# Linear attention in three parts: scores of a pair of blocks, outputs of the preceding pair, projections of the next; W_o's pieces by single chunks

## The chip, the cores and the metric

The kernel runs on one core of a Trainium2 chip. The metric is the device time of one execution in microseconds (us). Engines are named TensorE (PE in the profile; PEld is its weight load), VectorE (DVE), ScalarE (ACT), GpSimd (POOL) and SyncE (SP, which here only issues DMAs).

## The reference

One step of a hybrid decoder layer, in float32. A prompt of 2048 tokens and 8 decoded tokens pass through a normalisation and one combined projection. One half of the projected columns feeds sliding-window attention, the other half gated linear attention. Their outputs go through W_o, are added to the input, and a SwiGLU feed-forward layer follows.

```python
def gla_chunked(q, k, v, log_a, s0):
    """S_t = diag(a_t) S_{t-1} + k_t^T v_t, o_t = q_t S_t, chunk by chunk"""
    ...
    def step(S, inp):
        qc, kc, vc, ac = inp
        b = jnp.cumsum(ac, axis=2)
        o_inter = jnp.einsum('nhtd,nhdv->nhtv', qc * jnp.exp(b), S)
        diff = b[:, :, :, None, :] - b[:, :, None, :, :]
        decay = jnp.exp(jnp.where(causal[:, :, None], diff, -jnp.inf))
        scores = jnp.einsum('nhtd,nhsd,nhtsd->nhts', qc, kc, decay)
        o = o_inter + jnp.einsum('nhts,nhsv->nhtv', scores, vc)
        b_last = b[:, :, -1:, :]
        S = (jnp.exp(b_last[:, :, 0, :, None]) * S
             + jnp.einsum('nhsd,nhsv->nhdv', kc * jnp.exp(b_last - b), vc))
        return S, o

def finish(x, o_attn, o_gla, r_gla, gla_norm_g, w_o, ffn_norm_g, w_gate, w_up, w_down):
    g = rmsnorm(o_gla, gla_norm_g).reshape(N, T, GLA_WIDTH) * jax.nn.silu(r_gla)
    h = x + jnp.concatenate([o_attn, g], axis=-1) @ w_o
    z = rmsnorm(h, ffn_norm_g)
    return h + (jax.nn.silu(z @ w_gate) * (z @ w_up)) @ w_down
```

There are 4 heads with 64 key and 128 value columns.

## The kernel before

The program has five stages, one after another: sliding-window attention (to about 405 us of the span), gated linear attention (about 405 to 750), the W_o product with the second normalisation (about 727 to 937), gate and up products, and the down product. The last two use Strassen's seven products. A float32 product is made of three matmuls with split operands (`mm3`, L105 to L109): `split` (L94 to L96) makes a high part on ScalarE and the remainder on VectorE.

All instructions of an engine run in the order in which they were placed when the program was built. The framework places them by a simulated timeline (L1443, `schedule_with_timeline_sim`): whatever can start first goes first, and of several candidates the one that stands earlier in the program. At run time each engine keeps that order and waits at its head. SyncE's DMA issues are such a queue too, and so are GpSimd's instructions. Tiles live in pools with a fixed number of buffers (`bufs`); a tile whose buffer is still being read waits for it.

Linear attention works on pairs of 128-token blocks, pp = 0 to 7. Two functions did the work, and the loop at L955 to L959 called `gla_b(pp)`, then a piece of the decoded tokens' work (`next(dec)`), then `front_b(pp + 1)`.

- `front_b(pp)`: the projections of a pair. It loads the pair's normalised input `zT` (2 MB, L682, two halves in turn), makes q and k (`ps_qk`, 96 matmuls of 256 columns), the gates (`ps_g`) with their running sum `Bt` (L730), and the values v (`ps_v`, 48 matmuls of 512 columns, L743). It also loads r, the output gate made in the first stage (L754).
- `gla_b(pp)`, first half: the scores. Seven levels (`LEVELS`, 64 down to 1). In each, VectorE subtracts the running sum at a boundary (L797), ScalarE takes the absolute value and exponential (L798, L799), GpSimd multiplies q into a block-diagonal operand `bd` (L811, two instructions), VectorE multiplies k into E (L812), TensorE makes the level's scores (`ps_l`, L816), and ScalarE (L821) or a masked copy of VectorE (L826) puts them into `AT`. Then come the diagonal `dg` (L834 to L836), q with decay `eB` (L838, L841), its last column `ebl`, and the decayed and transposed keys `kdN` (L844 to L853).
- `gla_b(pp)`, second half: the outputs, block by block. `po` sums AT times v (L865) and eB times the running state `Sbd` (L868); `pst` makes the state's addition (L873), which VectorE applies (L880). VectorE adds the diagonal (`ob`, L886), ScalarE squares (L891), GpSimd multiplies by r (L892) and takes the inverse root (`rstd`, L115), ScalarE scales (L896), TensorE transposes (`ps_m`, L900), and the result goes to DRAM as `mix_d` (L903).

W_o is split into high and low parts inside the linear attention, and stored in DRAM (`wo_d`) for the next stage. `split_wo(i, behind)` (L769) splits the raw piece loaded by its last call, writes it, and loads the next. It was called in levels 1 and 5 of pairs 1 to 5, each piece two chunks of 128 rows by 512 columns; its ScalarE instruction is ordered behind the level's exponential (L799). Its pool has one buffer for the raw piece and one for the result.

The next stage loads `wo_d` as soon as its space is free (L1026; part of it overlaps `zT`, which the last `ps_v` reads), the mixed outputs (`mr`, L1016) and the residual input `h` (L1021; its buffers lie where tiles of the linear attention lay). `ps_wo` has four accumulators, each read by L586 together with h.

Of the kernel before, what the change touches and what calls it, by code (L numbers as in the profile page):

```python
# [10 lines left out]
F32 = mybir.dt.float32  # L11
# [9 lines left out]
P = 128  # L21
# [30 lines left out]
def hymba_kernel(ctx: ExitStack, tc: tile.TileContext, I, O, X=None, phases=3):  # L52
# [521 lines left out]

    def load_wo(wr, k0, dh):

        cols = slice(dh * 512, dh * 512 + 512)
        v = wr.rearrange("p (k n) -> p k n", k=2)
        if k0 >= 4:
            return [(v, w_o[k0 * P:(k0 + 2) * P, cols].rearrange("(k p) n -> p k n", p=P))]  # L580
        return [(v[64 * h:64 * h + 64], w_o[h * 256 + k0 * 64:h * 256 + (k0 + 2) * 64, cols]
                 .rearrange("(k p) n -> p k n", p=64)) for h in range(2)]

# [8 lines left out]
    with ExitStack() as ph:  # L592
# [4 lines left out]
        dp = pool(ph, "b_dec", 1)  # L597
        lp = pool(ph, "b_lm", 1)
        gtp = pool(ph, "b_gt", 2)
# [42 lines left out]
        lmask = pad.tile([P, len(LEVELS) * 64], U8, name="lmask")  # L642
        lm = lp.tile([P, 528], F32, name="lm")[:, 0:len(LEVELS) * 64]
        nc.sync.dma_start(lm, I["c_lmask"])
# [32 lines left out]
        def front_b(pp):  # L677
# [55 lines left out]
            def values():  # L733
                vs, rs = [], []
                toks = [(0, P), (P, P)] + ([(256, ND)] if pp == 0 else [])
                for c0, n in toks:
                    ps = acc.tile([P, 512], F32, tag="acc", name="ps_v")
                    v = wk.tile([P, 512], F32, tag="v", name="v", bufs=4)
                    if n == P:
                        for k in range(KD):  # L740
                            mm3(ps, nT[:, 0, k, c0:c0 + n], nT[:, 1, k, c0:c0 + n], WV[:, 0, k], WV[:, 1, k],
                                k == 0, k == KD - 1)
                        nc.scalar.copy(v, ps)  # L743
                    else:
                        for k in range(KD):
                            for hl in range(2):
                                nc.tensor.matmul(ps[:40], nTdec[:, k], WV[:, hl, k], start=k == 0 and hl == 0,
                                                 stop=k == KD - 1 and hl == 1)
                        nc.scalar.copy(v[:n], ps[32:40])
                        nc.vector.tensor_tensor(v[:n], ps[:n], v[:n], ALU.add)  # L750
                    vs.append(v)
                    if n == P:
                        r = wl.tile([P, 512], F32, tag="r", name="r", bufs=4)
                        nc.sync.dma_start(r, r_d[2 * pp + c0 // P])  # L754
                        rs.append(r)
                return vs, rs

            la, Bt = gates()
            vs, rs = values()
            if pp == 0:  # L760
# [3 lines left out]
                nc.sync.dma_start(vdec_d, vs[2][:ND])  # L764
            live[pp] = (qT, kTt, Bt, vs, rs)

        raw_wo = []

        def split_wo(i, behind):  # L769


            if raw_wo:
                wr, dh, k0 = raw_wo.pop()
                hl = wop.tile([P, 2, 2, 512], F32R, tag="hl", name="wohl")
                with tc.issue_after(behind.ins):
                    split(hl[:, 0], hl[:, 1], wr.rearrange("p (k n) -> p k n", k=2))
                nc.sync.dma_start(wo_d[dh][:, :, k0:k0 + 2], hl.bitcast(F32))
            if i < 8:
                dh, k0 = i // 4, 2 * (i % 4)
                wr = wop.tile([P, 1024], F32, tag="wr", name="wro")  # L780
                for dst, src in load_wo(wr, k0, dh):
                    nc.sync.dma_start(dst, src)
                raw_wo.append((wr, dh, k0))

        def gla_b(pp):
            qT, kTt, Bt, vs, rs = live.pop(pp)

# [3 lines left out]
            for li, H in enumerate(LEVELS):  # L791
# [8 lines left out]

                if li in (1, 5) and 2 <= 2 * pp + li // 5 <= 10:
                    split_wo(2 * pp + li // 5 - 2, grown)
                bd = bds[nbd[0] % 3]
# [32 lines left out]
            nc.vector.tensor_copy(dg, ps[:, 0:8])  # L836
            eB = wl.tile([P, 2, 256], F32, tag="eB", name="eB", bufs=1)
            nc.scalar.activation(eB, Bt, AF.Exp, scale=1.0 / 16)  # L838
# [11 lines left out]
            for g in range(4):  # L850
                nc.tensor.transpose(ps[:, g * P:(g + 1) * P], kdf[:, g * P:(g + 1) * P], ident)
            kdN = wl.tile([P, 4, P], F32, tag="kdN", name="kdN", bufs=1)
            nc.scalar.copy(kdN.rearrange("p g t -> p (g t)"), ps)  # L853
            eBf = eB.rearrange("p a t -> p (a t)")
            for c in range(2):
# [97 lines left out]
        front_b(0)  # L953
        dec = decode_b()
        for pp in range(NB // 2):  # L955
            gla_b(pp)
            next(dec, None)
            if pp + 1 < NB // 2:
                front_b(pp + 1)  # L959
        for p in range(2):  # L960
            for h in range(2):
                nc.sync.dma_start(O["gla_state_prompt"][0, 0, 2 * p + h], Sbd[64 * h:64 * h + 64, p, h * P:(h + 1) * P])
# [484 lines left out]
```

## Time and profile before

| | us |
|---|---|
| median of 3 runs | 2285.05 (2284.72 to 2285.94) |
| the profiled execution | 2284.49 |
| its span, first to last instruction | 2282.5 |
| TensorE busy in the span | 2206.6 (97%) |
| VectorE, ScalarE, GpSimd busy | 1567.7, 1009.3, 625.3 |
| mean granted TensorE clock | 0.986 |

Times in the trace are counted from the first instruction. A row of the view by stretches has the stretch, its length, the busy time of TensorE, its weight load, VectorE, ScalarE and GpSimd, each with a number of instructions, the granted clock of TensorE as a share of full speed, the mean busy share of 16 DMA engines, and GB/s. A row of the timeline has start, duration, engine, line, operation, tiles and count, and in brackets the idle time of that engine before it with what ended it. A group's row ends with busy time and mean duration in ns, then the idle time before its instructions and the releasers. One `mm3` is three rows (L107, L108, L109). "q" behind an engine's name is its queue of DMA issues.

### The profile page before, as it was taken

Reading aid. Unit: us, or ns where it says so; the run is one execution under the profiler, and the core shown is the slowest. Engines: PE = TensorE matmul, PEld = TensorE weight load, DVE = VectorE, ACT = ScalarE, POOL = GpSimd, SP = SyncE. Lnnn points to the kernel's source line nnn. Section 1 sums busy time; section 2 is a strip of 40 time slices with the busy share of each in tenths; the row PEclk is TensorE's granted clock in tenths of the full one; section 3 lists DMA queues with packets and bytes.
Section 4 is the critical chain, followed back from the end, with each engine's and each line's share of the span. In section 5 each row is a group of like instructions: output and inputs, shape, how many; then the busy total and the mean of one; then the engine's idle time right before and its main releaser. Section 6 shows DMA issues by size and latency. Waiting matters only on the chain.

```text
span 2282.5 us, 34902 instructions
## 1 busy us (share of the span) xinstructions
PE 2206.6 (97%) x12697; PEld 1908.8 (84%) x12697; DVE 1567.7 (69%) x3076; ACT 1009.3 (44%) x2259; POOL 625.3 (27%) x706
## 2 busy tenths in 40 slices
PE   8999998899998999999999999999999899999997
PEld 6888887688897788688888889999999878787886
DVE  6787888567766466776666667676676675747486
ACT  5666777465565334332333333333333333434342
POOL 2443433455465133211111111011110122222222
PEclk9999999899999999999999999999999999999999
DMA  7323334245424889944242366233333377878777
GB/s 236 120 77 103 108 104 163 91 132 187 144 88 188 303 291 314 320 137 127 81 124 81 114 222 240 89 107 97 94 103 93 126 200 172 216 171 227 162 203 239
DMA packets 211992, 364.75 MB, mean 160 GB/s; under 512 B 15683, under 2 KB 129116, under 8 KB 208732
## 3 DMA queue, kind: packets, MB, share of 16 engines
q1 hardware_dynamic: 174764, 259.05, 34.7%
q0 software_dynamic: 37056, 103.47, 17.8%
q8 instruction: 100, 1.64, 0.3%
q14 instruction: 72, 0.59, 0.1%
HBM read 211.24 MB, written 152.29 MB: 159 GB/s over the span
## 4 chain that ended last, share of the span: by engine, by line
PE 82%; DMA 5%; DVE 5%; issue 3%; POOL 2%; ACT 2%; SPq 0%; POOLq 0%; DVEq 0%; ACTq 0%
PE ps_b L108 8%; PE ps_b L107 8%; PE ps_b L109 8%; PE ps_c L108 5%; PE ps_c L107 5%; PE ps_c L109 5%; PE ps_a L108 5%; PE ps_a L107 5%; PE ps_a L109 5%; PE ps_d L107 3%; PE ps_d L108 3%; PE ps_d L109 3%; PE ps_wo L107 3%; PE ps_wo L109 3%; PE ps_wo L108 2%
## 5 line engine op out<-in xcount | busy, mean ns | idle before, releaser
L109 PE MATMUL ps_b<-z,whl 128*128 128x258 f32 (+1 forms) x792 | 253.6, 320 | 2.1 <-DVE whl L96 2.1
L107 PE MATMUL ps_b<-z,whl 128*128 128x258 f32 (+1 forms) x792 | 254.3, 321 | 1.2 <-ACT whl L95 1.2
L108 PE MATMUL ps_b<-z,whl 128*128 128x258 f32 (+1 forms) x792 | 254.5, 321 | 0.0
L95 ACT CAST dm<-mr 128x384 fp32r<-128x384 f32 (+1 forms) x224 | 108.1, 488 | 190.6 <-PE ps_b L109 100.6
L108 PE MATMUL ps_a<-z,whl 128*128 128x258 f32 (+1 forms) x528 | 169.4, 321 | 0.0
L108 PE MATMUL ps_c<-z,whl 128*128 128x258 f32 (+1 forms) x528 | 169.4, 321 | 0.0
L109 PE MATMUL ps_a<-z,whl 128*128 128x258 f32 (+1 forms) x528 | 169.2, 320 | 0.0
L109 PE MATMUL ps_c<-z,whl 128*128 128x258 f32 (+1 forms) x528 | 169.1, 320 | 0.0
L107 PE MATMUL ps_c<-z,whl 128*128 128x258 f32 (+1 forms) x528 | 168.9, 320 | 0.2 <-DMA z<-zc_d_P 0.2
L107 PE MATMUL ps_a<-z,whl 128*128 128x258 f32 (+1 forms) x528 | 169.0, 320 | 0.0
L109 PEld LDWEIGHTS ps_b<-z,whl 128*128 128x128 f32 x792 | 149.6, 189 | 14.5 <-DVE whl L96 2.5
L107 PEld LDWEIGHTS ps_b<-z,whl 128*128 128x128 f32 x792 | 149.7, 189 | 13.0 <-ACT whl L95 1.3
L108 PEld LDWEIGHTS ps_b<-z,whl 128*128 128x128 f32 x792 | 149.6, 189 | 11.9
L96 DVE TENSOR_TENSOR dm<-mr,dm 128x384 fp32r<-128x384 f32 (+1 forms) x224 | 115.4, 519 | 61.4 <-ACT dm L95 61.4
L95 ACT CAST whl<-wrg 128x512 fp32r<-128x512 f32 x132 | 81.6, 620 | 155.7 <-PE ps_b L109 81.2
L983 DVE TENSOR_TENSOR gu<-ps_c,gu 128x512 f32<-128x512 f32 (+1 forms) x130 | 77.9, 600 | 56.7 <-PE ps_c L109 56.1
L96 DVE TENSOR_TENSOR whl<-wrg,whl 128x512 fp32r<-128x512 f32 x132 | 90.8, 689 | 36.6 <-ACT whl L95 36.2
L811 POOL TENSOR_TENSOR bd<-E,qTb 64x256 f32<-64x256 f32 x112 | 103.2, 922 | 44.3 <-DVE ebl L840 15.7
L1282 POOL DMA_DIRECT2D md_d<-m x22 | 15.6, 711 | 363.5 <-DVE m L1245 363.5
L95 ACT CAST whl<-sy 128x512 fp32r<-128x512 f32 x88 | 54.6, 620 | 132.2 <-PE ps_b L109 84.9
L107 PEld LDWEIGHTS ps_c<-z,whl 128*128 128x128 f32 x528 | 100.0, 189 | 8.5 <-issue 0.6
L107 PEld LDWEIGHTS ps_a<-z,whl 128*128 128x128 f32 x528 | 100.0, 189 | 7.9
(399 smaller groups left out, 6684.7 us busy)
## 6 DMA issues: line engine op xcount, KB each, us to landing
mr<-md_d SPq DMA_DIRECT2D x24, 1344.0 KB
zc_d_P<-zhl POOLq DMA_DIRECT2D x56, 512.0 KB, 6.4
z<-zc_d_P SPq DMA_DIRECT2D x14, 2048.0 KB
wrg<-in_w_gate_dram SPq DMA_DIRECT2D x44, 512.0 KB
wrg<-in_w_up_dram SPq DMA_DIRECT2D x44, 512.0 KB
nT_d<-nT SPq DMA_DIRECT2D x16, 1024.0 KB
zT<-nT_d SPq DMA_DIRECT2D x8, 2048.0 KB
h_d<-gu POOLq DMA_DIRECT2D x48, 256.0 KB, 4.7
```

Source lines behind the costliest of these rows:

```text
L95: nc.scalar.copy(h, src)
L96: (eng or nc.vector).tensor_tensor(l, src, h.bitcast(F32), ALU.subtract)
L107: nc.tensor.matmul(ps, lh, rh, start=start, stop=False, skip_group_check=more)
L108: nc.tensor.matmul(ps, lh, rl, start=False, stop=False, skip_group_check=more)
L109: nc.tensor.matmul(ps, ll, rh, start=False, stop=stop, skip_group_check=more)
L811: nc.gpsimd.tensor_tensor(bv[rows, h], E5[rows, :, :, 1], qv[rows, :, :, 1], ALU.mult)
L983: nc.vector.tensor_tensor(out, a, b, ALU.add)
L1282: nc.gpsimd.dma_start(md_d[sb][g][:, :, q, fp - GROUPS[g][0], :], src.rearrange("p (m t) -> p m t", m=4))
```

## The change

`gla_b` is cut in two. `levels_b(pp)` keeps the scores with dg, eB, ebl and kdN, and starts with the loads of r. `out_b(pp)` has the outputs. The loop calls `levels_b(pp)`, `out_b(pp - 1)`, the decoded tokens' piece, and `front_b(pp + 1)`; `out_b(7)` follows the loop. v has 6 buffers instead of 4, eB and kdN two instead of one. The raw level mask `lm` uses a buffer of r's tag, and its pool is gone. W_o is split in 16 pieces of one chunk instead of 8 of two, in levels 1, 3 and 5 of pairs 1 to 5 and levels 1 and 3 of pair 6.

```diff
-    def load_wo(wr, k0, dh):
+    def load_wo(wr, k, dh):
...
-        if k0 >= 4:
-            return [(v, w_o[k0 * P:(k0 + 2) * P, cols].rearrange("(k p) n -> p k n", p=P))]
-        return [(v[64 * h:64 * h + 64], w_o[h * 256 + k0 * 64:h * 256 + (k0 + 2) * 64, cols]
-                 .rearrange("(k p) n -> p k n", p=64)) for h in range(2)]
+        if k >= 4:
+            return [(wr, w_o[k * P:(k + 1) * P, cols])]
+        return [(wr[64 * h:64 * h + 64], w_o[h * 256 + k * 64:h * 256 + (k + 1) * 64, cols]) for h in range(2)]
...
-        lp = pool(ph, "b_lm", 1)
...
-        lm = lp.tile([P, 528], F32, name="lm")[:, 0:len(LEVELS) * 64]
+        lm = wl.tile([P, 512], F32, tag="r", name="lm", bufs=4)[:, 0:len(LEVELS) * 64]
...
-                    v = wk.tile([P, 512], F32, tag="v", name="v", bufs=4)
+                    v = wk.tile([P, 512], F32, tag="v", name="v", bufs=6)
...
-                    if n == P:
-                        r = wl.tile([P, 512], F32, tag="r", name="r", bufs=4)
-                        nc.sync.dma_start(r, r_d[2 * pp + c0 // P])
-                        rs.append(r)
-                return vs, rs
+                return vs
...
-                wr, dh, k0 = raw_wo.pop()
-                hl = wop.tile([P, 2, 2, 512], F32R, tag="hl", name="wohl")
+                wr, dh, k = raw_wo.pop()
+                hl = wop.tile([P, 2, 512], F32R, tag="hl", name="wohl")
                 with tc.issue_after(behind.ins):
-                    split(hl[:, 0], hl[:, 1], wr.rearrange("p (k n) -> p k n", k=2))
-                nc.sync.dma_start(wo_d[dh][:, :, k0:k0 + 2], hl.bitcast(F32))
-            if i < 8:
-                dh, k0 = i // 4, 2 * (i % 4)
-                wr = wop.tile([P, 1024], F32, tag="wr", name="wro")
+                    split(hl[:, 0], hl[:, 1], wr)
+                nc.sync.dma_start(wo_d[dh][:, :, k], hl.bitcast(F32))
+            if i < 16:
+                dh, k = i // 8, i % 8
+                wr = wop.tile([P, 512], F32, tag="wr", name="wro")
...
-        def gla_b(pp):
-            qT, kTt, Bt, vs, rs = live.pop(pp)
+        done = {}
+
+        def levels_b(pp):
+
+            qT, kTt, Bt, vs = live.pop(pp)
+            rs = []
+            for c in range(2):
+                r = wl.tile([P, 512], F32, tag="r", name="r", bufs=4)
+                nc.sync.dma_start(r, r_d[2 * pp + c])
+                rs.append(r)
...
-                if li in (1, 5) and 2 <= 2 * pp + li // 5 <= 10:
-                    split_wo(2 * pp + li // 5 - 2, grown)
+                if li in (1, 3, 5) and 0 <= 3 * (pp - 1) + li // 2 <= 16:
+                    split_wo(3 * (pp - 1) + li // 2, grown)
...
-            eB = wl.tile([P, 2, 256], F32, tag="eB", name="eB", bufs=1)
+            eB = wl.tile([P, 2, 256], F32, tag="eB", name="eB", bufs=2)
...
-            kdN = wl.tile([P, 4, P], F32, tag="kdN", name="kdN", bufs=1)
+            kdN = wl.tile([P, 4, P], F32, tag="kdN", name="kdN", bufs=2)
             nc.scalar.copy(kdN.rearrange("p g t -> p (g t)"), ps)
+            done[pp] = (AT, dg, eB, ebl, kdN, vs, rs)
+
+        def out_b(pp):
+
+            AT, dg, eB, ebl, kdN, vs, rs = done.pop(pp)
...
         for pp in range(NB // 2):
-            gla_b(pp)
+            levels_b(pp)
+            if pp:
+                out_b(pp - 1)
             next(dec, None)
             if pp + 1 < NB // 2:
                 front_b(pp + 1)
+        out_b(NB // 2 - 1)
```

More of the change, by code (lines that the diff above doesn't have):

```diff
@@ L573, in hymba_kernel @@
     w_o = I["w_o"][0]
-    def load_wo(wr, k0, dh):
+    def load_wo(wr, k, dh):
         cols = slice(dh * 512, dh * 512 + 512)
-        v = wr.rearrange("p (k n) -> p k n", k=2)
-        if k0 >= 4:
-            return [(v, w_o[k0 * P:(k0 + 2) * P, cols].rearrange("(k p) n -> p k n", p=P))]
-        return [(v[64 * h:64 * h + 64], w_o[h * 256 + k0 * 64:h * 256 + (k0 + 2) * 64, cols]
-                 .rearrange("(k p) n -> p k n", p=64)) for h in range(2)]
+        if k >= 4:
+            return [(wr, w_o[k * P:(k + 1) * P, cols])]
+        return [(wr[64 * h:64 * h + 64], w_o[h * 256 + k * 64:h * 256 + (k + 1) * 64, cols]) for h in range(2)]
     def add_h(h, n, dh, ps):
@@ L733, in values @@
             def values():
-                vs, rs = [], []
+                vs = []
                 toks = [(0, P), (P, P)] + ([(256, ND)] if pp == 0 else [])
@@ L751, in values @@
                     vs.append(v)
-                    if n == P:
-                        r = wl.tile([P, 512], F32, tag="r", name="r", bufs=4)
-                        nc.sync.dma_start(r, r_d[2 * pp + c0 // P])
-                        rs.append(r)
-                return vs, rs
+                return vs
             la, Bt = gates()
-            vs, rs = values()
+            vs = values()
             if pp == 0:
@@ L764, in front_b @@
                 nc.sync.dma_start(vdec_d, vs[2][:ND])
-            live[pp] = (qT, kTt, Bt, vs, rs)
+            live[pp] = (qT, kTt, Bt, vs)
         raw_wo = []
@@ L772, in split_wo @@
             if raw_wo:
-                wr, dh, k0 = raw_wo.pop()
-                hl = wop.tile([P, 2, 2, 512], F32R, tag="hl", name="wohl")
+                wr, dh, k = raw_wo.pop()
+                hl = wop.tile([P, 2, 512], F32R, tag="hl", name="wohl")
                 with tc.issue_after(behind.ins):
-                    split(hl[:, 0], hl[:, 1], wr.rearrange("p (k n) -> p k n", k=2))
-                nc.sync.dma_start(wo_d[dh][:, :, k0:k0 + 2], hl.bitcast(F32))
-            if i < 8:
-                dh, k0 = i // 4, 2 * (i % 4)
-                wr = wop.tile([P, 1024], F32, tag="wr", name="wro")
-                for dst, src in load_wo(wr, k0, dh):
-                    nc.sync.dma_start(dst, src)
-                raw_wo.append((wr, dh, k0))
-        def gla_b(pp):
-            qT, kTt, Bt, vs, rs = live.pop(pp)
+                    split(hl[:, 0], hl[:, 1], wr)
[3 more added lines that the diff above has]
+                wr = wop.tile([P, 512], F32, tag="wr", name="wro")
+                for dst, src in load_wo(wr, k, dh):
+                    nc.sync.dma_start(dst, src)
+                raw_wo.append((wr, dh, k))
+        done = {}
[6 more added lines that the diff above has]
+                rs.append(r)
             AT = ATs[pp % 2]
```

## The prediction

> **What bounds the kernel now.** I read the page first: which engine is full, and over the whole span or in stages.
>
> ```profile
> span 2282.5 us, 34902 instructions
> PE 2206.6 (97%) x12697; PEld 1908.8 (84%) x12697; DVE 1567.7 (69%) x3076; ACT 1009.3 (44%) x2259; POOL 625.3 (27%) x706
> ```
>
> TensorE is full nearly everywhere, so a change that leaves its work alone can win only its idle time and its time at a lowered clock. The second view is the busy time by stretch, over the linear attention and what follows. The columns are stretch, length, busy time of each engine with instruction counts, granted clock, DMA share, GB/s.
>
> ```profile
> 434.00:683.00 249.00, 239.27 (x1702) 214.78 (x1700) 171.85 (x302) 147.02 (x363) 140.26 (x129) 0.99 0.40 130
> 683.00:727.00 44.00, 35.72 (x215) 30.24 (x214) 30.06 (x52) 24.31 (x59) 28.21 (x28) 0.92 0.53 205
> 727.00:762.00 35.00, 31.95 (x151) 24.87 (x150) 13.43 (x28) 12.13 (x33) 5.13 (x5) 0.95 0.50 182
> 762.00:937.00 175.00, 175.00 (x823) 142.35 (x822) 113.81 (x170) 65.44 (x109) 54.28 (x65) 1.00 0.91 300
> ```
>
> The first row is the steady state (pairs 0 to 6): 249 - 239.27 = 9.73 us idle. The second is the last pair, with nothing left to project: 8.28 us idle. The third is the start of the W_o product: 3.05 us. From 762 TensorE has no idle time at all, so whatever is won earlier passes on. Idle time to be won: 21.06 us. The clock is the other part; the same view in short stretches:
>
> ```profile
> 540.00:550.00 10.00, 7.82 (x47) 6.68 (x45) 9.93 (x17) 9.46 (x26) 5.97 (x6) 1.00 0.51 157
> 550.00:560.00 10.00, 10.00 (x76) 10.00 (x76) 4.89 (x8) 5.78 (x11) 8.14 (x10) 0.83 1.04 340
> ...
> 717.40:724.20 6.80, 6.78 (x32) 6.58 (x32) 2.49 (x4) 2.46 (x5) 3.63 (x4) 0.50 1.03 411
> 755.00:762.00 7.00, 4.22 (x16) 3.50 (x17) 6.03 (x9) 4.03 (x6) 0.55 (x1) 0.76 1.04 403
> ```
>
> Lost to the clock: 0.17 x 10 = 1.7, 0.5 x 6.8 = 3.4 and 0.24 x 7 = 1.7 us, 6.8 in all, each behind an idle spell. The whole pool is 21.06 + 6.8 = 27.9 us.
>
> Third, the groups of instructions in 434 to 683 say which wait it is (busy, mean ns | idle before, releaser).
>
> ```profile
> L816 PE MATMUL ps_l<-bd,E 128*128 128x128 f32 x352 | 48.1, 281 | 4.9 <-POOL bd L811 4.7
> ...
> L865 PE MATMUL po<-v,AT 128*128 128x128 f32 x96 | 15.5, 285 | 4.6 <-DVE AT L826 4.6
> ```
>
> Two waits make up the steady loss. The outputs (L865) wait for the last level's masked copy (L826), once a pair: they are issued right behind the scores that they need. The level products (L816) wait for GpSimd's operand (L811).
>
> **Steady state.** With outputs one pair late, AT, dg, eB, ebl, kdN and v of a pair are finished a whole level stage before L865 reads them. The 4.6 us go: -4.6. A wait that could follow is AT's reuse: two AT tiles, and levels of pair pp+2 write what outputs of pair pp read, but those stand ahead in program order. v gets 6 buffers instead of 4, eB and kdN 2 instead of 1: these cover the longer life.
>
> The wait of L816 goes in part. Its largest case (GpSimd, then TensorE):
>
> ```profile
> 545.55 1.47 POOL L841 TENSOR_TENSOR eB<-eB,qTb 128x512 f32<-128x512 f32 x1 [3.38 <-DVE rs_v L114]
> 546.99 1.19 POOL L115 TENSOR_TENSOR rs_r<-rs_v,nhalf 128x4 f32<-128x4 f32 x1
> 548.15 4.20 POOL L811 TENSOR_TENSOR bd<-E,qTb 64x256 f32<-64x256 f32 x5
> 549.94 1.90 PE L816 MATMUL ps_l<-bd,E 128*128 128x128 f32 x8 [2.18 <-POOL bd L811]
> ```
>
> The first operand of the next pair's levels stands behind eB and the norm of the previous output (L115), which itself waited. The doubled eB unties eB from the output that still reads it; L892 and L115 stay in the same in-order queue among the L811s, and more of them now fall inside a level stage. Between nothing (0) and all (-4.9) I take half: -2.4. The 1.7 us of clock behind that stall I take at half: -0.8.
>
> By the Trainium skill, "TensorE: Matmul & The Clock Gate" (Part 1: The HAM clock gate), the clock halves after a whole idle window of about 3.4 us. The 0.50 row behind the 3.41 us wait (below) agrees; the 0.83 row follows a stall of only 2.18 us, and there the trace decides. By the page alone that 0.8 would be left out of the sum.
>
> **The last pair and the start of W_o.** TensorE, then SyncE's queue:
>
> ```profile
> 702.75 1.50 PE L816 MATMUL ps_l<-bd,E 128*128 128x128 f32 x12
> 704.08 0.61 PE L865 MATMUL po<-v,AT 128*128 128x128 f32 x4
> ...
> 706.50 0.44 PE L873 MATMUL pst<-v,kdN 128*64 128x128 f32 x4
> ...
> 710.14 1.13 PE L816 MATMUL ps_l<-bd,E 128*128 128x128 f32 x8 [1.23 <-issue]
> 712.87 1.13 PE L816 MATMUL ps_l<-bd,E 128*128 128x128 f32 x8 [1.60 <-DVE AT L826]
> 717.42 0.48 PE L900 MATMUL ps_m<-ident,r 128*128 128x128 f32 x1 [3.41 <-ACT r L896]
> ...
> 725.47 0.71 PE L865 MATMUL po<-v,AT 128*128 128x128 f32 x4 [1.08 <-DVE AT L826]
> 727.14 0.58 PE L107 MATMUL ps_wo<-WO,mt 128*128 128x512 f32 x1
> 757.77 0.50 PE L107 MATMUL ps_wo<-WO,mt 128*128 128x512 f32 x1 [3.05 <-ACT mt L95]
> ```
>
> ```profile
> 702.94 2.57 SPq L1026 DMA_DIRECT2D WO<-wo_d  x4
> ...
> 749.27 0.33 SPq L903 DMA_DIRECT2D mix_d<-mob  x1
> 749.78 0.84 SPq L1021 DMA_DIRECT2D h<-in_x_prompt_dram  x2
> ```
>
> The last projection ends at 702.75; W_o's load starts then (its space is the projections'), and the product 24.4 us later. In between stand only pair 7's levels, chained over four engines, and one block's output of pair 6: 7.3 us of the 8.28 idle. After the change the outputs of pairs 6 and 7 both stand behind the last levels. One block's output holds TensorE from 704.08 to 706.94, some 2.8 us, so about 5.6 us of pair 6 become filler where TensorE idles, and the 3.41 us wait, which drags 3.4 us of half clock, should break up. Then SyncE: the residual loads (L1021) stand behind the last block's mix_d write (749.27), and their lateness costs the 3.05 us and 1.7 us of clock. Outputs of pair 7 remain the end of a chain, so this may stay. Pool here: 8.28 + 3.05 + 3.4 + 1.7 = 16.4. Bounds: none of it, or all; I take half, -8, nearest to the 5.6 us of filler plus a part of the clock.
>
> **W_o by single chunks.** Before, 8 splits of 1024 columns; after, 16 of 512.
>
> ```profile
> L95 ACT CAST wohl<-wro x8: 1030/1036/1045, 477.1 to 631.5; 128x1024 fp32r<-128x1024 f32 x8
> L96 DVE TENSOR_TENSOR wohl<-wro,wohl x8: 1211/1213/2297, 478.6 to 632.6; 128x1024 fp32r<-128x1024 f32 x8
> L95 ACT CAST zhl<-t 128x512 fp32r<-128x512 f32 x32 | 19.6, 618 | 33.5 <-DMA zc_d_P<-zhl 26.5 <-DVE t L980 7.0
> L96 DVE TENSOR_TENSOR zhl<-t,zhl 128x512 fp32r<-128x512 f32 x32 | 21.8, 687 | 15.0 <-ACT zhl L95 15.0
> ```
>
> ScalarE: 16 x 0.618 - 8 x 1.036 = +1.6 us; VectorE: 16 x 0.687 - 8 x 1.213 = +1.3 us, beside 102 and 77 idle us in the first stretch: nothing. SyncE issues 8 more writes and 12 more loads at about 0.6 us (the L782 row below), +12 us of a queue; what stands behind are zT, lr and mix transfers, each wanted much later. The bytes are the same. The cover is the distance between a raw load and its split, and it shrinks: one piece buffer and one result buffer, and 11 of 16 splits now come two levels behind their load. Before, with four levels:
>
> ```profile
> 505.43 0.56 SPq L682 DMA_DIRECT2D zT<-nT_d  x1
> 509.29 0.62 SPq L782 DMA_DIRECT2D wro<-in_w_o_dram  x1
> 519.98 1.04 ACT L95 CAST wohl<-wro 128x1024 fp32r<-128x1024 f32 x1 [3.42 <-DMA wro<-in_w_o_dram]
> 520.93 0.62 ACT L846 ACTIVATE kd<-kd 128x512 f32<-128x512 f32 x1
> ```
>
> A piece queued behind zT (2 MB) held ScalarE 3.42 us, with the pair's decayed keys (L846) and thereby its outputs behind it. Bounds: 0, if half-sized pieces land in time, and 11 x 3.42 = 38 us. One such wait in 8 splits is 0.43 us each; 16 of them are 7 us of ScalarE, of which I let about 2 reach TensorE, as most of a stall is taken up by ScalarE running ahead of GpSimd: +2. This is the term I know least.
>
> **Moves that I cost at nothing.**
>
> ```profile
> SPq L754 <- PE ps_m L900: 56.2, 8, 25.8
> ```
>
> r's loads go from the values to the head of the levels; SyncE stood up to 25.8 us before such a load waiting for a buffer (total, times, longest), and r is wanted a pair later now. lm shares r's buffers; the left-hand tiles shift by a few KB, so the first loads may wait for other tiles of the preceding stage. I see no row that prices it, and leave 0 with a bound of 2 us either way.
>
> **Sum.** -4.6 - 2.4 - 0.8 - 8 + 2 = -13.8. The profiled execution took 2284.49 us, 0.56 under the median of the runs: 2270.7 by it, 2271.3 by the median. I say 2271.
>
> **The rivals.** *Late W_o pieces, slower than before.* The 3.42 us wait is the row for it, the DMA share of 0.40 at 130 GB/s over 434 to 683 the one against. It decides once the 11 close splits cost TensorE over 15.8 + 4.6 = 20.4 us, 1.9 each; at two thirds of the full price, 25 us, the kernel takes 2284.5 - 15.8 + 25 = 2294. *A new wait in the levels, no change.* GpSimd and VectorE now mix a pair's outputs into the next one's levels:
>
> ```profile
> POOL rs_r L115 <- DVE rs_v L114: 22.7, 10, 15.3
> L811 POOL TENSOR_TENSOR bd<-E,qTb x112: 712/865/1743, 420.4 to 719.1; 64x256 f32<-64x256 f32 x112
> L812 DVE TENSOR_TENSOR E<-E,kTb x56: 409/529/1529, 421.5 to 716.9; 128x256 f32<-128x256 f32 x56
> ```
>
> If every one of 7 pairs had the 2.18 us stall of 549.94 the cost would be 15 us and the time 2284; for it speaks that L115 waits up to 15.3 us at the head of GpSimd's queue, and L812's spread from 409 to 1529 ns; against, that the next pair's projections and the last pair's outputs can be ordered in between. The Trainium skill, "SBUF - State Buffer" (SBUF: two separate sides), has VectorE operations with two SBUF inputs and GpSimd operations that read SBUF lock each other out for a whole instruction; that spread agrees, and the rule speaks for this rival. *All of it won:* 2284.5 - 27.9 = 2257. That the change doesn't do what it says is possible too: program order is only a priority, and the planner may place outputs where they were; that is the no-change case again.
>
> **How the numbers follow.** A measurement of this kernel tells a change of about 0.2% (4.6 us) from none. Chances: forecast, 2262 to 2280, 0.50; nearly all won, under 2262, 0.12; no change, 2280.5 to 2289.6, 0.18; slower, 0.20, nearly all of it the late pieces. Faster 0.62, same 0.18, slower 0.20. The range 2259 to 2292 leaves out some 0.05 below and 0.14 above; the forecast's own is 2262 to 2280.
>
> **What would show it.** Right: L865 with hardly any wait for L826; between the last projection and the first W_o product no idle spell of 3 us and the clock at 1.00; projections ending some 10 us earlier than 702.75, counted from the same start. Wrong: ScalarE idle before L95 wohl with the DMA as releaser, at two places a pair; L816 with more than 10 us of idle behind L811; the W_o product still 3 us late behind its residual.

## The result and the profile after

The changed kernel takes 2287.75 us (median of 20 runs, 2283.95 to 2291.98), the kernel before 2284.82 (20 runs): a ratio of 1.0014 (95% interval 1.0008 to 1.0021), so 3 us slower, which is less than the 0.2% that counts as a change here, and 17 us above the forecast. The profiled execution has 2286.16 us and a span of 2284.4.

The kernel after, by stretches, with the columns of the prediction's first such view:

```profile
434.00:683.00 249.00, 240.86 (x1649) 211.51 (x1648) 171.62 (x310) 143.31 (x362) 144.55 (x131) 0.99 0.40 126
683.00:727.00 44.00, 35.60 (x219) 30.54 (x219) 25.00 (x48) 25.34 (x63) 24.74 (x25) 0.90 0.45 172
727.00:762.00 35.00, 33.12 (x168) 26.30 (x167) 15.18 (x29) 12.04 (x33) 6.91 (x6) 0.97 0.59 220
762.00:937.00 175.00, 174.95 (x821) 141.93 (x821) 114.64 (x169) 67.09 (x110) 54.59 (x65) 1.00 0.92 304
```

Idle in the last pair is 44 - 35.60 = 8.40 us (8.28 before) at a clock of 0.90 (0.92); at the start of W_o 1.88 us (3.05). What TensorE waits for between 434 and 762 (total us, times, longest), first before:

```profile
PE po L865 <- DVE AT L826: 5.7, 5, 1.7
PE ps_l L816 <- POOL bd L811: 5.7, 7, 2.2
PE ps_m L900 <- ACT r L896: 3.4, 1, 3.4
PE ps_wo L107 <- ACT mt L95: 3.1, 1, 3.1
PE ps_l L816 <- DVE AT L826: 1.6, 1, 1.6
PE ps_l L816 <- issue: 1.2, 1, 1.2
```

and after:

```profile
PE ps_l L817 <- POOL bd L812: 11.0, 12, 3.5
PE ps_l L817 <- DVE AT L827: 4.2, 3, 1.7
PE ps_wo L107 <- ACT mt L95: 1.6, 1, 1.6
PE ps_kd L852 <- POOL kd L848: 0.8, 2, 0.5
PE ps_m L906 <- ACT kdN L854: 0.2, 1, 0.2
```

The wait of po is gone, and so is nearly all of ps_m's. The level products' waits grew by 6.7 us (8.5 with the 1.2 us put down to issue, to 15.2). That is two thirds of the 10.4 us by which the waits of po, ps_m and ps_wo fell (5.7 + 3.2 + 1.5). The largest case is in the last pair (after, timeline of TensorE, then of GpSimd):

```profile
712.63 1.16 PE L817 MATMUL ps_l<-bd,E 128*128 128x128 f32 x8 [1.60 <-POOL bd L812]
714.58 1.16 PE L817 MATMUL ps_l<-bd,E 128*128 128x128 f32 x8 [0.79 <-POOL bd L812]
716.66 1.16 PE L817 MATMUL ps_l<-bd,E 128*128 128x128 f32 x8 [0.92 <-POOL bd L812]
721.34 2.07 PE L817 MATMUL ps_l<-bd,E 128*128 128x128 f32 x8 [3.52 <-POOL bd L812]
```

```profile
714.60 2.00 POOL L812 TENSOR_TENSOR bd<-E,qTb 64x256 f32<-64x256 f32 x2
716.68 1.67 POOL L898 TENSOR_TENSOR r<-ob,r 128x512 f32<-128x512 f32 x1
718.32 1.19 POOL L115 TENSOR_TENSOR rs_r<-rs_v,nhalf 128x4 f32<-128x4 f32 x1
719.47 1.81 POOL L812 TENSOR_TENSOR bd<-E,qTb 64x256 f32<-64x256 f32 x2
```

GpSimd does r and the inverse root of pair 6's last output (2.9 us) between two operands of pair 7's levels, and TensorE stands for 3.52 us. No matmul of pair 6 fills the gap, for its two po blocks started at 692.97 and 701.54, and the last ps_v at 708.8: the placement had drawn them into the last projection. Elsewhere too an output was moved by far less than a pair: over the 16 blocks, the first product of po starts between 4.1 us earlier and 11.1 us later than before, while the levels of one pair and of the next start some 30 to 45 us apart.

Idle time is not what the kernel lost. The same work, from the last ps_v of pair 0's prompt tokens to the 104th ps_wo, before and then after:

```profile
426.00:762.18 336.18, 315.12 (x2114) 276.20 (x2113) 217.71 (x384) 187.52 (x462) 177.18 (x165) 0.98 0.44 148
```

```profile
423.90:764.20 340.30, 321.83 (x2115) 278.26 (x2114) 218.00 (x392) 186.88 (x469) 181.37 (x165) 0.97 0.44 146
```

Idle fell from 21.06 to 18.47 us (-2.6). But TensorE was busy 6.7 us longer with the same matmuls. Of that, half clock is 0.4: the three stretches after, shown here, hold 14.36 us of busy time, those before 13.6, and half of the difference counts.

```profile
442.10:445.50 3.40, 3.40 (x18) 3.40 (x17) 1.57 (x3) 0.84 (x2) 1.28 (x1) 0.51 0.26 77
602.60:606.00 3.40, 3.40 (x17) 3.40 (x18) 2.25 (x3) 1.05 (x3) 2.00 (x2) 0.50 0.35 129
718.60:728.90 10.30, 7.56 (x35) 7.54 (x36) 4.95 (x9) 2.85 (x7) 8.80 (x9) 0.50 1.03 410
```

The other 6.3 us lie in the distances from one matmul's start to the next one's (idle and half clock taken off, summed by kind), above all ps_qk 85.2 to 87.6, pst 11.8 to 13.7, ps_l 49.0 to 50.5 and ps_bo 2.5 to 3.4. With idle and busy time together this stretch is 4.1 us longer. Ahead of it, pair 0's projections run 1.8 us shorter, at a clock of 0.88 against 0.83 (before, then after):

```profile
371.60:426.00 54.40, 42.46 (x231) 36.53 (x230) 37.45 (x91) 31.78 (x78) 18.34 (x19) 0.83 0.42 137
```

```profile
371.30:423.90 52.60, 40.40 (x231) 34.26 (x230) 37.15 (x91) 31.28 (x77) 18.21 (x19) 0.88 0.42 137
```

4.1 - 1.8 - 0.3 (the earlier start) = 2.0; the spans of the two profiled executions differ by 1.9.

### The profile page after: what moved, and what is told of

Its sections match the earlier page's. It is cut to its first block, busy times and chain, and to the rows that moved or that the text cites. A ratio compares the mean times of both kernels' runs of the same rounds, so it can differ in the third digit from the quotient of the medians.

```text
span 2284.4 us, 34959 instructions
## 1 busy us (share of the span) xinstructions
PE 2211.4 (97%) x12697; PEld 1907.0 (83%) x12697; DVE 1568.7 (69%) x3084; ACT 1009.4 (44%) x2267; POOL 630.3 (28%) x706
## 4 chain that ended last, share of the span: by engine, by line
PE 83%; DVE 6%; DMA 4%; issue 3%; ACT 2%; POOL 1%; SPq 1%; POOLq 0%; DVEq 0%; ACTq 0%
PE ps_b L108 8%; PE ps_b L107 8%; PE ps_b L109 8%; PE ps_c L108 5%; PE ps_c L107 5%; PE ps_c L109 5%; PE ps_a L108 5%; PE ps_a L107 5%; PE ps_a L109 5%; PE ps_d L107 3%; PE ps_d L108 3%; PE ps_d L109 3%; PE ps_wo L107 3%; PE ps_wo L109 2%; PE ps_wo L108 2%
```

## The experiments

Differences in us are ratio times 2285, each ratio to runs of the kernel before on the same chip; an interval is about ±2 us. "Base" is the kernel with all of the change but the reordering. "Busy" and "idle" are TensorE's in one profiled execution, over the same work as above. "Clock" is the part of "busy" that half clock cost (half of the busy time in the stretches at 0.50), so "busy" less "clock" is the busy time at full clock. "Runs" counts, over the same work, how often TensorE goes over to pst's products from any others.

| label | kernel | median | ratio (95%) | busy | idle | clock | runs |
|---|---|---|---|---|---|---|---|
| | before | 2284.82 | 1 | 315.1 | 21.1 | 6.8 | 28 |
| | after | 2287.75 | 1.0014 (1.0008, 1.0021) | 321.8 | 18.5 | 7.2 | 36 |
| e1 | before, W_o single | 2282.84 | 0.9993 (0.9984, 1.0002) | 315.4 | 21.2 | 8.5 | 26 |
| e2 | base | 2279.07 | 0.9976 (0.9968, 0.9985) | 312.5 | 18.5 | 5.1 | 26 |
| e3 | after, no GpSimd in out_b | 2283.97 | 0.9999 (0.9990, 1.0007) | 319.5 | 16.2 | 6.5 | 35 |
| e4 | after, outputs held | 2286.65 | 1.0006 (0.9997, 1.0015) | 322.0 | 18.2 | 6.5 | 39 |
| f1 | after, grouped | 2280.99 | 0.9986 (0.9978, 0.9995) | 314.4 | 17.9 | 6.3 | 21 |
| f2 | after, tail held | 2289.89 | 1.0030 (1.0019, 1.0041) | 321.2 | 19.9 | 6.2 | 37 |
| f3 | e1 with eB, kdN doubled | 2279.29 | 0.9981 (0.9973, 0.9990) | 315.3 | 18.1 | 8.0 | 26 |
| f4 | base, no GpSimd in outputs | 2291.03 | 1.0028 (1.0019, 1.0037) | 319.5 | 23.3 | 8.8 | 26 |
| g1 | base, grouped | 2277.05 | 0.9966 (0.9952, 0.9979) | 312.3 | 16.8 | 4.4 | 25 |
| g2 | before, grouped | 2273.89 | 0.9950 (0.9937, 0.9962) | 311.9 | 12.4 | 3.3 | 26 |
| g3 | f1, no GpSimd in out_b | 2275.92 | 0.9965 (0.9952, 0.9977) | 312.7 | 14.6 | 4.5 | 21 |
| h1 | after, decoded piece first | 2281.70 | 0.9983 (0.9974, 0.9991) | 318.3 | 14.7 | 5.3 | 33 |
| h2 | base, decoded piece first | 2283.45 | 0.9988 (0.9979, 0.9996) | 316.6 | 18.7 | 7.8 | 26 |
| h3 | after, W_o at levels 0, 2, 4 | 2285.52 | 0.9999 (0.9990, 1.0007) | 320.0 | 18.3 | 5.4 | 36 |
| h4 | base, W_o at levels 0, 2, 4 | 2286.30 | 1.0001 (0.9992, 1.0010) | 316.1 | 21.2 | 9.0 | 25 |
| i1 | h1, grouped | 2278.41 | 0.9975 (0.9965, 0.9985) | 316.5 | 14.0 | 6.0 | 22 |
| i2 | e1, grouped | 2280.14 | 0.9985 (0.9976, 0.9994) | 311.6 | 17.7 | 3.5 | 24 |

### First: W_o, the buffers, or the order

The theory then was P: the placement put the outputs only a little later, and their GpSimd and VectorE work now stands ahead of the next levels' operands. The rivals were W (late W_o pieces) and L (another layout and plan).

**e1**, the kernel before with only the edits of `load_wo` and `split_wo` and their call (the call is shown):

```diff
-                if li in (1, 5) and 2 <= 2 * pp + li // 5 <= 10:
-                    split_wo(2 * pp + li // 5 - 2, grown)
+                if li in (1, 3, 5) and 0 <= 3 * (pp - 1) + li // 2 <= 16:
+                    split_wo(3 * (pp - 1) + li // 2, grown)
```

> The kernel before with one part of the change alone: W_o in 16 single-chunk pieces, in the levels where the change puts them; order and buffers as before. Theory P (the planner): the changed kernel loses because outputs moved only a little, and their GpSimd and VectorE work now stands in front of the next pair's level operands; W_o's pieces have little to do with it. Then this kernel is within 2 us of the kernel before (2284.8). Theory W (W_o's pieces): ScalarE waits for late pieces (9.8 us in 6 waits in the changed kernel's profile, 3.4 us in 1 before) and the splits on VectorE take 17.9 instead of 12.0 us, and this delays the levels. Then this kernel takes 2287 to 2290, with some 10 us of such waits and more than 12 us of idle before the level products.

2282.84 us: the pieces cost nothing that can be measured, though ScalarE waited for them 15.2 us in ten cases. Theory W falls.

**e2**, the base: e1 with the buffers and the mask; `gla_b`, the loop and the loads of r as they were.

```diff
-        lp = pool(ph, "b_lm", 1)
...
-        lm = lp.tile([P, 528], F32, name="lm")[:, 0:len(LEVELS) * 64]
+        lm = wl.tile([P, 512], F32, tag="r", name="lm", bufs=4)[:, 0:len(LEVELS) * 64]
...
-                    v = wk.tile([P, 512], F32, tag="v", name="v", bufs=4)
+                    v = wk.tile([P, 512], F32, tag="v", name="v", bufs=6)
...
-            eB = wl.tile([P, 2, 256], F32, tag="eB", name="eB", bufs=1)
+            eB = wl.tile([P, 2, 256], F32, tag="eB", name="eB", bufs=2)
...
-            kdN = wl.tile([P, 4, P], F32, tag="kdN", name="kdN", bufs=1)
+            kdN = wl.tile([P, 4, P], F32, tag="kdN", name="kdN", bufs=2)
```

> The change without its reordering: single-chunk W_o pieces, six buffers for v, two for eB and kdN, the raw mask among r's buffers; levels and outputs of a pair together in one function as before, r loaded with the values. Theory P: 2282 to 2286, as the order of the outputs is what costs, and untying eB may win 1 or 2 us; the output products still wait for the last masked copy, some 5 us in all. Theory W: 2287 to 2290, as in the run before. A third theory, L (the new place of tiles or a reshuffled plan, not any one part): anything over 2287 here while the first run stays at 2285.

2279.07 us, 5.5 us under before and below every range that was given for it. Between this kernel and the changed one lies nothing but the reordering (with the place of r's loads): 8.7 us. The level products' wait for GpSimd's operand, 11.0 us in the changed kernel, is next to nothing here:

```profile
PE ps_l L813 <- POOL bd L808: 0.4, 1, 0.4
```

**e3**, the changed kernel with GpSimd's part of the outputs on VectorE and ScalarE:

```diff
-                nc.gpsimd.tensor_tensor(r, ob, r, ALU.mult)
-                rr = rstd(ss, P, 1.0 / P, 4)
+                nc.vector.tensor_tensor(r, ob, r, ALU.mult)
+                rr = rstd_fast(ss, P, 1.0 / P, 4)
```

> The changed kernel with the outputs' two GpSimd instructions a block (product with r, inverse root) given to VectorE and ScalarE, so that GpSimd has the levels almost to itself. Theory P: the level products' wait for GpSimd falls from 11.0 us to 5 or less and the time to 2281 to 2285. Theory W: the wait stays near 11 us and the time at 2287 or more, since the operands are late for ScalarE's or VectorE's sake.

3.4 us less than after, with the idle time 2.3 us and the busy time 2.3 us lower. The wait for GpSimd's operand fell from 11.0 to 2.9 us. It fits P as far as it goes.

**e4**, the overlap that the prediction had in mind made real: the outputs' first block issued behind the next pair's level 1, the second behind level 4 (`marks` holds the last level product of each pair and level).

```diff
+                if pp + 1 < NB // 2:
+                    held.enter_context(tc.issue_after(marks[pp + 1, (1, 4)[c]].ins))
```

> The changed kernel with the output matmuls of a pair's first block placed behind the second level of the next pair, and those of its second block behind the fifth level, so that the overlap that the change is named for really takes place; pair 7's outputs are free. If the overlap is worth what I forecast (outputs of pair 6 fill TensorE between the last levels), idle time after the last projection falls by 4 us or more and the time is 2272 to 2280. Theory P: the outputs' GpSimd and VectorE work stands in every level stage, the level products wait more (over 20 us in all) and the time is 2288 to 2296, though TensorE's idle time in the last pair falls. Theory W: no change, 2286 to 2289.

2286.65 us, level with before: above the 2272 to 2280 of the forecast and under the 2288 to 2296 of theory P. Outputs among the next levels are not worth what the forecast gave them.

**f3**, e1 with two buffers each of eB and kdN, and nothing else.

> The kernel before with W_o by single chunks and two buffers each of eB and kdN; the loop, the value buffers and the masks as they were. The kernel with these edits and six value buffers and the masks in r's buffer took 2279.07 us, the one with single chunks alone 2282.84 us. If eB and kdN bring the 3.8 us between them (outputs of the last pair and its kdN no longer wait for the pair ahead): 2279 to 2280 us. If the value buffers, or a plan that comes out otherwise, bring it: 2282 to 2284 us.

2279.29 us. TensorE's instructions come in the same order as in e2, and the time is the same: six value buffers and the mask in r's buffer do nothing that can be measured, while the doubled eB and kdN bring about 2.7 us over e1 (the two intervals overlap a little). The two profiles also say which figures repeat where the order is the same: at full clock busy time is 307.3 and 307.4 us, idle time 18.1 and 18.5, but the clock took 8.0 us from one execution and 5.1 from the other.

### Second: matmul steps, or the tail

Two theories for the 8.7 us: S, the busy time of shorter runs of po and pst, that is, of more steps from the one kind of product to the other; T, the last levels standing alone.

**f1**, in `out_b`:

```diff
                     if b > 0:
                         nc.tensor.matmul(po[:, p * 256:(p + 1) * 256], eBf[...], Sbd[:, p, :], ...)
-
+                for p in range(2):
+                    g = 2 * p + c
                     for h in range(2):
                         rows = slice(64 * h, 64 * h + 64)
                         nc.tensor.matmul(pst[rows, p * P:(p + 1) * P], kdN[:, g, rows], ...)
```

> The new kernel with one edit in the outputs: all six products of po first and then the four of pst, where the new kernel issues three, two, three, two. Theory S (the new order's loss of 8.7 us against the same kernel without the reordering is mostly TensorE time that no wait shows: between the last value product of the first pair and the 104th W_o product the steps from po to pst and back, 25 x 0.30 us and 14 x 0.2 us, against 18 and 10 there): the steps fall to about 16 and 4, some 4 us are saved, 2283 to 2285 us. Theory T (the loss is in the tail, where the sixth pair's outputs are done before the last projection ends and the last levels stand alone): no more than 1 us, 2287 to 2288 us.

2280.99 us, 6.4 us less and more than S gave, and nearly all of it is busy time (321.8 to 314.4; idle 18.5 to 17.9). One block, undivided, in the changed kernel and then with the grouping (timeline):

```profile
692.97 0.61 PE L871 MATMUL po<-v,AT 128*128 128x128 f32 x4
693.42 0.60 PE L874 MATMUL po<-Sbd,eB 128*128 128x256 f32 x2
693.95 0.44 PE L879 MATMUL pst<-v,kdN 128*64 128x128 f32 x4
694.32 0.71 PE L871 MATMUL po<-v,AT 128*128 128x128 f32 x4
694.87 0.60 PE L874 MATMUL po<-Sbd,eB 128*128 128x256 f32 x2
695.39 0.44 PE L879 MATMUL pst<-v,kdN 128*64 128x128 f32 x4
695.76 0.50 PE L107 MATMUL ps_v<-WV,zT 128*128 128x512 f32 x1
```

```profile
689.35 0.61 PE L871 MATMUL po<-v,AT 128*128 128x128 f32 x4
689.79 0.60 PE L874 MATMUL po<-Sbd,eB 128*128 128x256 f32 x2
690.23 0.61 PE L871 MATMUL po<-v,AT 128*128 128x128 f32 x4
690.67 0.60 PE L874 MATMUL po<-Sbd,eB 128*128 128x256 f32 x2
691.20 0.66 PE L880 MATMUL pst<-v,kdN 128*64 128x128 f32 x8
691.79 0.50 PE L107 MATMUL ps_v<-WV,zT 128*128 128x512 f32 x1
```

695.76 - 692.97 = 2.79 us against 691.79 - 689.35 = 2.44: one pair of steps between operands 128 and 64 wide costs 0.35 us, and no row shows it as idle. (The other blocks that stand undivided in these two kernels among projections take the same 2.79 and 2.44 us.) The Trainium skill, "TensorEngine Tiling (Array Packing)" (Key Properties), says that a change of the tiling mode drains TensorE. These rows fit that and give the price for this shape, though they show no drain as such.

**f2**, the changed kernel with one block held:

```diff
+                if pp == NB // 2 - 2 and c == 1:
+                    held.enter_context(tc.issue_after(marks[pp + 1, 0].ins))
```

> The new kernel with one thing held: the second block of the next to last pair's outputs is issued only behind the first level's product of the last pair, as it comes by itself in the kernel before. Theory T: these ten products and their four transpositions (about 2.8 us) then lie in the gaps of the last levels, where the new kernel has 6.8 us of idle time and 10.3 us at half clock between 712 and 729 us; the last value product comes some 3 us earlier, the last level product hardly later: 3 to 6 us won, 2282 to 2285 us. Theory S: nothing in the steady state changes, so 2287 to 2288 us.

2289.89 us, above both answers: theory T falls. The last value product comes 3 us earlier and the block's matmuls lie among pair 7's levels, as T had it, but so does the rest of the block. TensorE, then GpSimd:

```profile
708.11 1.16 PE L817 MATMUL ps_l<-bd,E 128*128 128x128 f32 x8 [2.35 <-POOL bd L812]
720.90 2.05 PE L817 MATMUL ps_l<-bd,E 128*128 128x128 f32 x8 [4.20 <-DVE rs_v L114]
```

```profile
716.52 1.26 POOL L903 TENSOR_TENSOR r<-ob,r 128x512 f32<-128x512 f32 x1
717.74 1.72 POOL L832 TENSOR_TENSOR qk<-qTb,kTb 128x512 f32<-128x512 f32 x1
720.89 1.01 POOL L115 TENSOR_TENSOR rs_r<-rs_v,nhalf 128x4 f32<-128x4 f32 x1 [1.43 <-DVE rs_v L114]
```

The inverse root waits 1.43 us at the head of GpSimd's queue, and TensorE's wait is 4.20 us instead of 3.52.

**f4**, the edit of e3 on the base.

> All of the change but the reordering (2279.07 us), with the outputs' product with r on VectorE and their reciprocal root on ScalarE and VectorE instead of GpSimd. The same edit took 3.8 us off the new kernel. Theory P (GpSimd's work for the outputs costs because the new order puts it ahead of the next pair's level operands): the order here has it behind them, so at most 1 us changes, 2278 to 2280 us. The rival: GpSimd's work for the outputs costs in either order, 3 to 4 us off, 2275 to 2276 us.

2291.03 us: both answers were wrong. The edit that takes 3.4 us off the changed kernel puts 12 on the base. Theory P cannot be the whole: what the same work costs depends on the order around it.

**g1, g2, g3**: the grouping on the base and on the kernel before, and f1 with the edit of e3.

> All of the change but the reordering (2279.07 us), and the outputs' six products of po ahead of the four of pst. On the new kernel the same edit took 6.8 us off. Theory S (a step from po to pst costs some 0.17 us above what the two products take, one back some 0.14 us, in any order): as issued there are 10 steps to pst and none back, against 18 and 10 without the grouping: 8 x 0.17 + 10 x 0.14 = 2.8 us off, 2275 to 2277 us. If grouping helped the new kernel only because its plan fell out otherwise: 2278 to 2281 us.

> The kernel before with the grouping alone. As issued 14 steps to pst and none back, against 19 and 9. Theory S: 5 x 0.17 + 9 x 0.14 = 2.1 us off, a ratio near 0.999. If it is the plan and not the steps: anything between 0.998 and 1.002, with the time of po and pst from start to start unchanged (29.8 and 11.8 us between the first pair's last value product and the 104th W_o product).

> The new kernel with the grouping (2280.99 us) and the outputs' GpSimd work on VectorE and ScalarE. Grouping alone leaves 13.5 us of waits of the level products, most of them for GpSimd's operand. Theory P (these waits are what is left of the reordering's loss): they fall by some 5 us, 2276 to 2278 us. The rival, by the run of this edit in the old order (2291.03 us, 12 us slower): VectorE takes the same work and makes the operands late in its place, 2281 us or more.

g1 gains 2.3 us, the amount that S gave, but by luck: its busy time stays (312.5 to 312.3), the idle time falls. g2 gains 11.4 where S gave 2.1, outside both answers, and is the fastest kernel of this study, with the reordering left out. The whole stretch, and its half clock:

```profile
427.40:751.70 324.30, 311.89 (x2115) 273.60 (x2114) 218.97 (x384) 184.94 (x462) 178.97 (x164) 0.99 0.45 153
709.30:716.10 6.80, 6.55 (x31) 6.33 (x32) 3.86 (x7) 3.73 (x8) 6.38 (x8) 0.50 1.02 409
```

Idle time fell by 8.7 us and busy time by 3.2. The 3.2 are the clock: half of 6.55 is 3.3 us, against 6.8 in the kernel before. At full clock busy time did not fall (308.3 to 308.6), so the steps bring nothing that shows here: the gain is idle time and clock, under an order written out anew. g3 is 4.8 us under f1, as P had it.

S counted the steps between po and pst alone. Counted with every neighbour ("runs"), the grouping takes away 15 runs in the changed kernel and 14 from e3 to g3; at 0.35 us each that is 5.3 and 4.9 us, and busy time at full clock fell by 6.5 and 4.8. In the base and the kernel before it takes away 1 and 2, as transpositions (ps_m) stand ahead of pst in po's place, and busy time at full clock rose by 0.5 and 0.3.

### Third: the reordering, or the order that was written out

O: late outputs as such cost. D: the order that the placement happened to write decides, whatever the reason that it was written. The decoded piece and the levels of W_o's splits were moved, in both loops; no instruction is added or removed.

```diff
+            next(dec, None)
             levels_b(pp)
             if pp:
                 out_b(pp - 1)
-            next(dec, None)
```

```diff
-                if li in (1, 3, 5) and 0 <= 3 * (pp - 1) + li // 2 <= 16:
+                if li in (0, 2, 4) and 0 <= 3 * (pp - 1) + li // 2 <= 16:
```

> The new kernel with the decoded tokens' piece called ahead of the levels instead of behind the outputs. No instruction is added or removed; the placement writes out another order. Theory O (late outputs as such cost): as the new kernel, 2286 to 2290 us. Theory D (the order that is written out decides, whatever the reason it was changed): anything from 2277 to 2292 us, and more than 2 us from 2287.75.

> All of the change but the reordering, with the decoded piece called ahead of the scores: the partner of the run before. Theory O: 2277 to 2281 us, and 6 to 11 us under its partner. Theory D: more than 2 us from 2279.07, and a distance to its partner of any sign.

> The new kernel with W_o's splits in levels 0, 2 and 4 instead of 1, 3 and 5. Theory O: 2286 to 2290 us. Theory D: more than 2 us away from 2287.75, to either side.

> All of the change but the reordering, with W_o's splits in levels 0, 2 and 4: the partner of the run before. Theory O: 2277 to 2281 us, 6 to 11 us under its partner. Theory D: more than 2 us from 2279.07, and a distance of any sign.

The moves changed the time by -7.1 (h1), +2.7 (h2), -3.4 (h3) and +5.7 us (h4). What the reordering costs is then, in five pairs: plain 8.7 (e2), decoded piece first -1.1, other levels -0.5, grouped 4.6 (f1, g1), without GpSimd -6.6 (e3, f4). The mean is 1.0, each difference known to some 3 us. O asked for 6 to 11 in both new pairs and falls as a statement on the time; D, which allowed almost any other value, is what is left.

The profiles show more, for one execution of each kernel. Read between 434 and 770 us, and in the order plain, decoded piece first, other levels and grouped, the reordering took the wait of po for AT from 9.1, 5.6, 3.8 and 6.5 us to none, 0.7, 0.3 and 1.3, and the wait of the level products for GpSimd's operand from 0.4, 4.5, 2.5 and 1.2 us to 11.0, 9.8, 11.4 and 9.1. So both the gain that was forecast and the rival's loss come with the reordering, whatever else the order is. It also added 7.2, 4.2, 7.5 and 0.2 us of busy time at full clock, and 2.3 without GpSimd: late outputs cost TensorE time unless the products are grouped. The runs of pst go with it in the three ungrouped orders (7 to 11 more, 2.5 to 3.9 us at 0.35), which leaves about half of the added time unexplained. Idle time and clock together changed by +2.1, -6.5, -6.5 and +3.0 us, and by -9.4 without GpSimd, and this part has no fixed sign.

**i1, i2**: the grouping on h1 and e1.

> The new kernel with the decoded piece ahead (ratio 0.9983 to the kernel before) and po's products ahead of pst's. A block that stands undivided takes 2.79 us without the grouping and 2.44 us with it; 16 blocks give at most 5.6 us, and as issued 13 steps to pst and 3 back remain of 25 and 14. If the steps are the cause: 3 to 5.5 us off, a ratio of 0.9960 to 0.9970. If the order written out is: any change between -8 and +4 us.

> The kernel before with W_o by single chunks (ratio 0.9993) and the grouping. As issued 10 steps to pst and none back, of 19 and 9. If the steps are the cause: 2 to 4 us off, 0.9975 to 0.9985. If the order written out is: any change between -8 and +4 us.

1.8 us less in both: for i1 less than the steps gave, for i2 at the edge of their range. But in i2 it is not the steps: its runs fell from 26 to 24, and its busy time at full clock rose by 1.2 us. In i1 they fell from 33 to 22 (3.9 us at 0.35), and it fell by 2.5. With these, the grouping was tried in six orders, and the median was lower in each: 6.4, 2.3, 11.4, 7.8 (e3 to g3), 1.8 and 1.8 us. The gains of about 2 us are within the uncertainty of a single comparison.

## Why the prediction was wrong, step by step

2287.75 us lies inside the range and on the other side of the forecast.

- *The outputs' wait, -4.6: right.* Between 434 and 762 po's wait went from 5.7 us to none, and L871 had no idle time at all.
- *Half of the level products' wait, -2.4: wrong in sign.* 5.7 us behind `bd` became 11.0, and 1.6 behind AT became 4.2. The second rival named this mechanism, GpSimd's and VectorE's output work inside the levels, and e2, e3 and f2 show it at work. The term's bounds, nothing and -4.9, left out that the wait could grow. The rival's time of 2284 leaves out the 2 us of W_o's pieces; with them it is 2286. The *0.8 of clock* behind it was not won: the clock term of the same work grew by 0.4.
- *The last pair and W_o's start, -8: the largest failure.* It rested on program order, "the outputs of pairs 6 and 7 both stand behind the last levels". The instruction order is made by a simulated timeline, as the text on the kernel says, and that had issued all but six of pair 6's po and pst products before the last projection ended. Measured: +0.1 us of idle in the last pair, -1.2 at W_o's start, and a last projection that started its last product 6 us later than before (708.8 against 702.5), where the prediction looked for 10 us earlier. Nor was the idea worth its price where it was made true (e4, f2): a block brings its VectorE and GpSimd work along as well as its matmuls.
- *W_o's pieces, +2: too dear.* e1 shows -1.6 (-3.7 to 0.5). ScalarE did wait for pieces, as feared (15.2 us in ten cases in e1, 9.8 us in six in the changed kernel), and no loss of time followed in e1. The VectorE price of 687 ns was too low for this place: on average 969 ns in e1 and 1122 ns in the changed kernel, whose rows are these:

```profile
L96 DVE TENSOR_TENSOR wohl<-wro,wohl 128x512 fp32r<-128x512 f32 x16 | 17.9, 1122 | 7.0 <-ACT wohl L95 6.7
L95 ACT CAST wohl<-wro 128x512 fp32r<-128x512 f32 x16 | 9.8, 611 | 9.8 <-DMA wro<-in_w_o_dram 9.8
```

- *The moves at nothing: right for the mask and the value buffers* (f3 against e2). What moving r's loads did is in no run by itself. The doubled eB, priced only through the level products' wait, and kdN, counted as cover, are worth some 2.7 us alone.
- *What the sum left out.* "A change that leaves its work alone can win only its idle time and its time at a lowered clock": the busy time went up by 6.7 us with the same matmuls, more than the idle time won. f1 shows that it can be had back by grouping po and pst (308.1 us at full clock, against 314.6 in the changed kernel and 308.3 before).
- *The uncertainty of the order itself.* Moves that change no instruction shifted the time by 2.7 to 7.1 us. The whole effect of the change, +3 us, is within that, so a sum of waits taken from the old order was unlikely to settle its sign. That the result lies inside the range is due to the range's width and not to the forecast.

What stays open is why a written order is good or bad. The rows name its waits one by one, but no run here moved one thing with the rest of the order held fixed, and the runs do not say how far the simulated times were off. Open too are the part of the added busy time that the steps do not explain, above all in ps_qk and ps_l, and why the edit of e3 costs the base 12 us.

## What to carry over

Where a planner writes the instruction order, look at the order that it writes before pricing a move by program order, and measure a few edits that do nothing: their spread is the least that a claimed gain must exceed. Count matmul steps as well as waits, and with every neighbour: busy time is not fixed work, and grouping products of one operand shape lowered it where it cut the number of runs, and not where it only changed the neighbour. Take the half clock off before reading a difference in busy time: with the same order it differed by 2.9 us from one execution to another. An output block that is to fill a gap brings the work of all its engines into that gap.

## What was not expected of the hardware

A step from products with 128-column operands to products with 64 and back costs 0.35 us of TensorE without any idle time in the trace. The half clock at 718.6 began when the last level product had ended only 0.8 us before (716.66 + 1.16 = 717.82), behind three shorter idle spells; those at 442.1 and 602.6 follow single spells of 0.93 and 1.68 us. The three half-clock stretches of the changed kernel last 3.4, 3.4 and 10.3 us. The Trainium skill, "TensorE: Matmul & The Clock Gate" (Part 1: The HAM clock gate), asks for a whole idle window of about 3.4 us ahead of it; these stretches do not agree, while the lengths come close to one, one and three such windows. VectorE's 512-column subtraction of W_o took 1122 ns on average in the changed kernel's linear attention and 969 in e1's, against the 687 of the row that the prediction took; no run here shows why.
